# A decoder trunk in split float32 on one core: buffers, weights, latents and keys moved by bytes, and two groups of spare transposes replaced by products in two halves

## The chip, the core and the metric

The kernel runs on one core of a Trainium2 chip. Five engines work side by side on a core: TensorE (PE in the profile; its weight loads are listed apart as PEld), VectorE (DVE), ScalarE (ACT), GpSimd (POOL) and SyncE (SP, which here issues the transfers). Operands lie in the core's SBUF memory, 128 partitions wide; TensorE accumulates into PSUM, eight banks of 512 float32 a partition. The metric is the device time of one execution in microseconds, as a median over runs.

## What is computed

A trunk of two layers over 256 positions of width 1024. Cut to what matters:

```python
for i in range(2):
    if i == 1:
        k_nope, k_rope, v = shared_kv(x, kv_w_down, kv_norm, kv_w_up, cos, sin)
    x = post_norm(x, 0.5 * swiglu(x, ffn1_w_in[i], ffn1_w_out[i]), ...)   # 1024 -> 2 x 2816 -> 1024
    mix = fox_mixer(x, ...) if i == 0 else mla_mixer(x, ...)              # 16 heads each
    x = post_norm(x, mix, ...)
    x = post_norm(x, 0.5 * swiglu(x, ffn2_w_in[i], ffn2_w_out[i]), ...)
    gate = sigmoid(x @ ple_w_gate[i] + ple_b_gate[i])
    x = post_norm(x, gate * (p[i] @ ple_w_proj[i]), ...)
```

All inputs are float32. Every weight is used once per execution and streams in from HBM.

## The kernel before

**Split products.** Each float32 operand is held as two rounded halves, high and low. `mm3` (line 605) issues three matmuls for each product: high by high, high by low, low by high, into one accumulator. Weights are loaded as raw tiles of 128 x 2048, and `Stream.split` (line 226) turns each into units of 1024 columns: ScalarE writes the high half, VectorE the low half, into one of ten slots `hl0` to `hl9`, or into a buffer lent for the time (`fs`, `qk`, `ota`, `otb`, `gb`). `place` (line 221) lays a unit into its slot, high half first, low half 1024 columns (4096 bytes) later. Keys named `fv` and the first layer's `pg` begin 48 columns (192 bytes) into their slot; all other keys begin at its start. `pump`, `extra`, `ahead` and `fill` decide when the next unit is split, from a running estimate of each engine's time (`busy`).

**Where the tiles lie.** The pool stacks its tiles in the order of their first use, each as large as its largest user. In bytes of a partition: ..., `xT` 16384, `rope` 1024, two `ss` of 32, `fs` 8448, `hl0` to `hl6` 8448 each, `P` 2 x 4096, `g4` 6 x 4096, `hl7` to `hl9`, `gb` 8448, `ts` 6144, `qk` 8576, `ota` 8448, `otb` 8448, small tiles, `PT` 6144, ..., `raw`. The start addresses of the kernel before, modulo 256 bytes, are: `xT` 160; `fs`, every `hl`, `P`, `g4`, `gb` and `qk` 224; `ota` and `otb` 96; `PT` 160. (8448 is 33 times 256; the two `ss` put 64 between `xT` and what follows; `qk`, of 2144 columns, is 33.5 times 256 and puts 128 between itself and what follows.)

**Stages in order**, with their places in the profiled span: first FFN (`ffn`, "cold", to 185 us), forgetting attention (`fox`, to 300), second FFN (to 484), gate (`ple`, to 509), FFN of layer 2 with the shared latent (`kv_down`, to 694), latent attention (`mla`, to 831), last FFN (to 1015), last gate. The order of work inside `fox` and `mla` is written out by hand in the lists `FOX` and `ORDER`.

**An FFN** has eleven chunks of 256 hidden columns. In a FFN that isn't the first, `H` (chunks 0 and 1) has x stationary (`xT`) and the weight `win` moving, 512 columns wide. `HT` (line 807) has the weight stationary and `xT` moving: 256 columns, as two runs of 128 (one for each half of the rows) 8192 bytes apart; 96 matmuls a chunk. Chunks 2 to 10 come in three groups of three. In the first chunk of each group, at its second step (k = 1, b = 0), `HT` calls `what` with the next bank: four transposes of 128 columns. They are real ones where there is something to turn (`T(0)`, `T(1)`, `ple_transpose`, `kv_transpose`), and in the first FFN's second and third group (chunks 5 and 8) they turn the identity into a bank that nobody reads (`spare`, line 720). After the first and the second group `sums` (line 865) multiplies the activated chunks by combined output weights: the activation, in one of the homes `fs`, `qk`, `ota`, `otb` (in this order), is stationary, the weight moves 512 wide; 21 matmuls a chunk, four chunks a call (two and three in the first FFN). `W` closes with the remaining chunks from `g4`.

**Elsewhere.** `fox`: values in `VA`, `VB`, `VC` (keys `fv`, `fvb`, `fvc`, moving against `xT`; `fvc` with a pitch of 272 columns), keys and queries in `ws` (weight stationary, `xT` moving), output in `O` (stationary `ota`, `otb`, moving `fo`). `mla`: query latent in `dq` (moving against `xT`), turned into `cqt` (in `gb`), rotary queries in `q_rope` (stationary `cqt`, moving `qr`), values in `V` (stationary `ckv` in `fs`, moving `kvv`), and for each head `gen` (line 1689): 6 matmuls with stationary `kvk` and moving `ckv`, 9 with stationary `qn` and moving `cqt`, both 2 x 128 columns; `QK` with the rotary key `kr` (in `fs` from column 1088) moving; output in `O` (stationary `otb`, `ota`, and `fs` for the last two heads).

Of the kernel before, what the change touches and what calls it, by code (L numbers as in the profile page):

```python
# [11 lines left out]
F32R = mybir.dt.float32r  # L12
# [132 lines left out]
class Stream:  # L145
# [74 lines left out]

    def place(self, key, slot):
        w = self.pool.tile([128, 2112], F32R, tag=slot, name=slot, bufs=1)
        c = 48 if moves(key) else 0
        return w[:, c : c + 2048].rearrange("p (i c) -> p i c", i=2)

    def split(self, half=False):
        self.later()
        nc = self.nc
        key = self.order[self.ready]
        g = group_of(key)  # L230
        while self.sums_left(key):
            self.add(g)
        src, parts, n = unit_of(key, self.raw[g], self.sums.get(g))
        if self.aside(key):
            w = self.pool.tile([128, 2, 512], F32R, tag="g4", name="g4", bufs=6)
        else:
            slot = self.slots.pop(0)
            self.slot_of[key] = slot
            w = self.place(key, slot)
        hi, lo = w[:parts, 0, :n], w[:parts, 1, :n]  # L240
        shape = src.shape
        if len(shape) == 3:
            hi = hi.rearrange("p (a b) -> p a b", b=shape[2])
            lo = lo.rearrange("p (a b) -> p a b", b=shape[2])
        elif len(shape) == 4:
            hi = hi.rearrange("p (a b c) -> p a b c", b=shape[2], c=shape[3])
            lo = lo.rearrange("p (a b c) -> p a b c", b=shape[2], c=shape[3])
        t = self.arrives[group_of(key)]
        self.act_t, self.dve_t = max(self.act_t, t), max(self.dve_t, t)

        def both():
            nc.scalar.activation(hi, src, AF.Copy)  # L252
            nc.vector.tensor_tensor(lo, src, hi.bitcast(F32), op=ALU.subtract)  # L253

        if key[0] == "pb":
            nc.gpsimd.memset(w[:, 0, :].bitcast(F32), 0.0)
            lo = w[32:33, 0, :n]
            both()
        elif half:
            nc.scalar.activation(hi, src, AF.Copy)  # L260
            self.busy(act=n)

            def rest():
                nc.vector.tensor_tensor(lo, src, hi.bitcast(F32), op=ALU.subtract)  # L264
                self.busy(dve=n)
                self.split_done(key, w)

            self.rest = rest
            return
        else:  # L270
            both()
        self.pair(n)
        self.split_done(key, w)

    def aside(self, key):
# [148 lines left out]
    return key  # L424


def moves(key):
    return key[0] == "fv" or key[:2] == ("pg", 0)


def unit_of(key, raw, sums=None):

    k, u = key[0], key[-1] % 2
    if k in ("win", "fv"):
        return raw.rearrange("p (k c) -> p k c", c=512)[:, 2 * u : 2 * u + 2, :], 128, 1024
    if k == "wiu":
        return raw[:, 1024 * u : 1024 * u + 1024], 128, 1024
    if k == "ws":
        i = key[-1]
        return ((raw, sums)[i // 2])[:, 1024 * u : 1024 * u + (512 if i == 3 else 1024)], 128, 512 if i == 3 else 1024  # L440
    if k == "fvc":
        n = 816 if key[-1] < 2 else 544
        return raw[:, n * u : n * u + n], 128, n
    if k in ("wout", "fvb", "fo", "pg", "pp", "mo", "qr"):
        return raw[:, 1024 * u : 1024 * u + 1024], 128, 1024
    if k in ("fk", "fq"):
        return raw.rearrange("p (k c) -> p k c", c=256)[:, :, 128 * u : 128 * u + 128], 128, 1024
    if k == "pb":
        return raw[0:1, 0:1024], 1, 1024
    if k == "kd":  # L450
        return raw[:, 640 * u : 640 * u + 640], 128, 640
    if k == "dq":
        return raw[:, 768 * u : 768 * u + 768], 128, 768
    if k == "qn":
        return raw[:, 512:1280], 128, 768
    if k == "kvv":
        return raw[:, 0:1024], 128, 1024
    if k == "kvk":
        return raw[:, 0:512], 128, 512
    raise KeyError(key)  # L460
# [50 lines left out]
class Trunk:  # L511
# [209 lines left out]
    def ffn(self, li, which, lni, kv=False, ple=False, at=None, cold=False, after=()):  # L721


        nc, S = self.nc, self.S
# [79 lines left out]

            return f

        def HT(c, gate, up, what=None):
            for half in range(2):
                ps = self.bank(*(up if half else gate))
                for u in range(2):  # L810
                    w = self.use(("wiu", li, which, c, 2 * half + u))
                    for kk, b in ((kk, b) for kk in range(4) for b in range(2)):
                        k = 4 * u + kk
                        if (half, k, b) == (0, 1, 0) and what:
                            what(self.bank(*up))
                        col = slice(256 * kk + 128 * b, 256 * kk + 128 * b + 128)
                        self.mm3(
                            ps[:, 256 * b : 256 * b + 256], lambda i: w[:, i, col], lambda i: self.xT[:, :, i, k, :],
                            (k, b) == (0, 0), (k, b) == (7, 1),
                        )  # L820
                if half == 0:
                    gt = self.room(c, summed)
                    nc.scalar.activation(gt, ps, AF.Silu)  # L823
                    S.busy(act=512)
            close(c, gt, ps)
# [123 lines left out]
        else:  # L949
# [13 lines left out]
        n = NCH  # L963

        turns = (
            None if cold else T(0),
            self.spare if cold else T(1),
            self.kv_transpose if kv else self.ple_transpose if ple else self.spare,
        )
        x = self.turn["h"] if cold else 1 - self.turn["h"]  # L970
        for i, group in enumerate((((1,) + GROUPS[0]) if cold else GROUPS[0],) + GROUPS[1:]):
            for c in group:
                for f in at.get(c, ()):
                    f()
                if c == 2:
                    S.lend("gb")
                if c == 8:
                    S.reclaim("gb")
                if c == 10:
                    S.check("gb")  # L980
                    self.load_gb(li, lni)
                if c == 10 and kv:
                    self.kv_transpose_rope()
                if i == 0 and c == group[0]:
                    banks = ("tr", self.turn["tr"]), ("tr", 1 - self.turn["tr"])
                    turn = turns[0] and (lambda _: turns[0](self.bank("h", 1 - x)))
                    HT(c, *banks, turn)
                else:
                    HT(c, ("h", x), ("h", 1 - x), turns[i] if c == group[0] else None)
            if i < 2:  # L990
                if i == 1 and kv:
                    self.flush()
                sums([c for c in summed if (c < 5 and (cold or c != 1)) == (i == 0)], ("h", x))
                x = 1 - x
            if i == 1:
                S.lend(*after)
                combine()
# [126 lines left out]
    def fox(self, li):  # L1124
        nc, S, a = self.nc, self.S, self.a
# [26 lines left out]
        def VC(t, at={}):  # L1152

            ps = self.bank("y")
            for k in range(8):
                if k in at:
                    at[k]()
                if k % 3 == 0:
                    w = self.use(("fvc", k // 3))
                c = 272 * (k % 3)  # L1160
                self.mm3(
                    ps[:, 0:272], lambda i: self.xT[:, t, i, k, :], lambda i: w[:, i, c : c + 272], k == 0, k == 7)
            if (t, 1) not in v:
                v[t, 1] = self.tl([128, 2, 512], F32R, "g4", 6)
            o = v[t, 1]
            nc.scalar.activation(ftok[:, t, 112:128], ps[:, 256:272], AF.Copy)
            self.parts(o[:, 0, 256:512], o[:, 1, 256:512], ps[:, 0:256])
# [26 lines left out]
        f, e, u, r, ab = (fs[fr, 256 * i : 256 * i + 256] for i in range(5))  # L1194
# [79 lines left out]
        qk = self.own([128, 2, 2, 512], F32R, "qk")  # L1274
# [200 lines left out]

    def kv_transpose_rope(self):
        nc = self.nc
        self.kr = self.kvt[:, 1088:1856].rearrange("p (i t c) -> p t i c", t=2, i=3)
        kr = [self.kr[:, :, i, :] for i in range(3)]
        b = self.bank("tr")  # L1480
        for t in range(2):
# [20 lines left out]
    def mla(self, li):  # L1502
# [3 lines left out]
            self.dma(qn, pbcast(a["mla_q_norm"][0], QR))  # L1506
        scale = float(192 ** -0.5)
        v = {}
        cqt = self.tl([128, 2, 2, 3, 128], F32R, "gb", 1)
        cqtok = self.tl([128, 2, 768], F32, "PT", 1)  # L1510
        S.reclaim("otb", "qk")
        home = {}
# [163 lines left out]

        def gen(h):
            if h == 0:
                o = self.own([128, 2, 1072], F32R, "qk")
                home["qk"] = o[:, :, 0:1024].rearrange("p w (t i s c) -> p w t i s c", t=2, i=2, s=2)  # L1680
            ps = self.bank("h")
            hp, s = h // 2, h % 2
# [252 lines left out]
```

## Time and profile before

| | |
|---|---|
| median of three runs | 1050.32 us (1049.77 to 1051.04) |
| the profiled execution's own time | 1049.6 us |
| its span in the profile | 1047.8 us |
| granted TensorE clock, mean of the span | 0.998 |
| HBM read | 200.55 MB, 192 GB/s over the span |
| matmuls | 7085 |

The profile is one execution; its span runs from the first to the last profiled instruction, 1.8 us shorter than that execution's own time. In the timeline a row merges instructions of one kind on one engine: start, length, engine, line, operation, result <- operands, partitions x columns of the moving operand, and how many. A matmul's record is longer than its turn, since the next one starts before it ends: a turn is the distance from one start to the next, so a group's mean turn is the distance from its row's start to the next row's start, over its count. The chain of waits gives start, length and count of pieces without that overlap. The trace shows no addresses: distances between operands come from the program, as given above.

### The profile page before, as it was taken

The numbers are of one execution on the slowest core, as the hardware profiler recorded it, in microseconds if no ns is written. First come the engines' busy times: TensorE is split into PE (matmuls) and PEld (weight loads), VectorE is DVE, ScalarE is ACT, GpSimd is POOL, SyncE is SP. The second block draws the span as 40 slices with busy tenths as digits, with TensorE's granted clock in tenths as the row PEclk, the third lists the DMA queues.
The fourth block names the chain that finished last, engine by engine and source line by source line (L and its number), as shares of the span: only waits on it lengthen the run. The fifth ranks groups of instructions, "written<-read, shape, count | busy, mean of one in ns | idle before, by whom it ended". The sixth has DMA issues, their size and how long they took to land.

```text
span 1047.8 us, 17555 instructions
## 1 busy us (share of the span) xinstructions
PE 1035.6 (99%) x7085; PEld 948.6 (91%) x7085; DVE 891.8 (85%) x1312; ACT 592.9 (57%) x901; POOL 58.0 (6%) x88
## 2 busy tenths in 40 slices
PE   9999999999999999999999999999999999999996
PEld 8999898899889999998899898988999889898986
DVE  5788977868898979978979899888887989889877
ACT  6555563666755555663565646646776564646541
POOL 0000000122300000000220000000000000000000
PEclk9999999999999999999999999999999999999999
DMA  7855586455636363673674545743445564555732
GB/s 281 305 191 188 185 298 243 162 168 169 216 128 246 121 252 125 241 282 132 236 260 151 195 169 190 270 142 112 145 156 179 183 214 162 200 190 176 271 125 81
DMA packets 37476, 202.74 MB, mean 193 GB/s; under 512 B 3970, under 2 KB 9874, under 8 KB 16532
## 3 DMA queue, kind: packets, MB, share of 16 engines
q1 hardware_dynamic: 37396, 201.63, 54.3%
q8 instruction: 55, 0.90, 0.3%
q14 instruction: 25, 0.20, 0.1%
HBM read 200.55 MB, written 1.06 MB: 192 GB/s over the span
## 4 chain that ended last, share of the span: by engine, by line
PE 95%; DVE 2%; ACT 1%; issue 1%; DMA 0%; SPq 0%; DVEq 0%; ACTq 0%
PE h L616 53%; PE y L616 29%; PE tr L616 10%; PE tr L620 2%; DVE hl L253 1%; PE h L620 1%; DMA raw<-in_w_dram 0%; PE tr L1375 0%; DVE ts L300 0%; DVE x L705 0%; DVE tr L1720 0%; ACT qk L629 0%; DVE PT L633 0%; DVE ts L306 0%; DVE raw L308 0%
## 5 line engine op out<-in xcount | busy, mean ns | idle before, releaser
L616 PE MATMUL h<-xT,hl 128*128 128x256 f32 x3144 | 366.1, 277 | 1.2 <-ACT hl L327 0.7
L616 PEld LDWEIGHTS h<-xT,hl 128*128 128x128 f32 x3144 | 362.0, 188 | 2.9 <-ACT hl L327 1.2
L253 DVE TENSOR_TENSOR hl<-raw,hl 128x1024 fp32r<-128x1024 f32 (+5 forms) x271 | 314.2, 1190 | 36.1 <-ACT hl L252 35.0
L252 ACT ACTIVATE hl<-raw 128x1024 fp32r<-128x1024 f32 (+5 forms) x271 | 267.8, 1027 | 70.6 <-DVE raw L308 41.3
L616 PE MATMUL y<-hl,g 128*128 128x512 f32 x336 | 78.6, 391 | 0.0
L616 PEld LDWEIGHTS y<-hl,g 128*128 128x128 f32 x336 | 62.5, 188 | 12.6
L616 PE MATMUL h<-hl,xT 128*128 128x512 f32 (+2 forms) x312 | 67.9, 371 | 0.0
L616 PEld LDWEIGHTS h<-hl,xT 128*128 128x128 f32 x312 | 54.9, 188 | 9.8
L616 PE MATMUL y<-hl,otb 128*128 128x512 f32 x219 | 58.0, 399 | 0.0
L264 DVE TENSOR_TENSOR hl<-raw,hl 128x1024 fp32r<-128x1024 f32 (+2 forms) x44 | 52.3, 1192 | 0.8 <-ACT hl L260 0.7
L616 PE MATMUL y<-hl,xT 128*128 128x512 f32 (+3 forms) x282 | 52.7, 334 | 0.0
L260 ACT ACTIVATE hl<-raw 128x1024 fp32r<-128x1024 f32 (+2 forms) x44 | 45.2, 1029 | 9.7 <-DVE raw L308 9.1
L629 ACT ACTIVATE xT<-tr 128x512 fp32r<-128x512 f32 x28 | 16.1, 597 | 58.9 <-PE tr L620 58.9
L616 PEld LDWEIGHTS y<-hl,xT 128*128 128x128 f32 x282 | 44.1, 188 | 4.6 <-ACT xT L629 0.4
L616 PEld LDWEIGHTS y<-hl,otb 128*128 128x128 f32 x219 | 39.8, 188 | 8.4 <-DVE otb L633 0.3
L616 PE MATMUL y<-hl,ota 128*128 128x512 f32 x177 | 46.8, 398 | 0.1
L700 POOL TENSOR_TENSOR rs<-ve,mhalf 128x1 f32<-128x1 f32 x16 | 15.1, 942 | 519.8 <-DVE ve L699 519.8
L616 PE MATMUL tr<-xT,hl 128*128 128x256 f32 x360 | 42.5, 277 | 0.0
L616 PEld LDWEIGHTS tr<-xT,hl 128*128 128x128 f32 x360 | 41.7, 188 | 0.4
L616 PEld LDWEIGHTS y<-hl,ota 128*128 128x128 f32 x177 | 32.7, 189 | 7.7 <-DVE hl L253 0.6
L823 ACT ACTIVATE P<-h 128x512 f32<-128x512 f32 x33 | 19.7, 596 | 33.0 <-PE h L616 32.6
L300 DVE TENSOR_TENSOR ts<-raw 128x1024 f32<-128x1024 f32 x29 | 35.4, 1222 | 0.6
(322 smaller groups left out, 1632.7 us busy)
## 6 DMA issues: line engine op xcount, KB each, us to landing
raw<-in_ffn_in_dram SPq DMA_DIRECT2D x85, 1024.0 KB, 5.0
raw<-in_ffn_out_dram SPq DMA_DIRECT2D x44, 1024.0 KB, 5.0
raw<-in_pg_dram SPq DMA_DIRECT2D x8, 1024.0 KB, 4.9
raw<-in_mo_dram SPq DMA_DIRECT2D x8, 1024.0 KB, 4.8
raw<-in_kq_dram SPq DMA_DIRECT2D x8, 640.0 KB, 4.2
gb<-in_ln_g_dram SPq DMA_DIRECT2D x8, 512.0 KB, 5.9
gb<-in_ln_b_dram SPq DMA_DIRECT2D x8, 512.0 KB, 7.5
raw<-in_fk_dram SPq DMA_DIRECT2D x4, 1024.0 KB, 5.6
```

The lines of the kernel that those rows point to most:

```text
L252: nc.scalar.activation(hi, src, AF.Copy)
L253: nc.vector.tensor_tensor(lo, src, hi.bitcast(F32), op=ALU.subtract)
L260: nc.scalar.activation(hi, src, AF.Copy)
L264: nc.vector.tensor_tensor(lo, src, hi.bitcast(F32), op=ALU.subtract)
L300: tt(s[:, 0:1024].rearrange("p (a b) -> p a b", b=512), r[:, 0:512][:, None, :].to_broadcast([128, 2, 512]), r[:, 512:1536].rearrange("p ( ...
L616: self.nc.tensor.matmul(out, lhsT, rhs, start=start, stop=stop)
L620: self.nc.tensor.transpose(out, in_, self.ident)
L629: self.nc.scalar.activation(hi, src, AF.Copy)
L700: nc.gpsimd.tensor_tensor(rs, ve, self.mhalf, op=ALU.pow)
L823: nc.scalar.activation(gt, ps, AF.Silu)
```

## The change

It has four parts. First, every unit of some keys begins further into its slot: 48 columns for `kvv`, `qr` and all `win` but the first FFN's, 32 for `fvb` and `fvc`, 36 for `kd`, 40 for `dq`; the columns of `fvc` are laid with a pitch of 320 where it was 272. Second, `cqt` begins 48 columns into `gb`, and `kr` 32 columns further into `fs`. Third, the `qk` tile is declared 2176 columns long where it was 2144 (its inner pitch stays 1072), so all tiles stacked behind it move by 128 bytes. Fourth, `spare` is no longer called from `HT`; in the first FFN's chunks 5 and 8 the matmul high by high of step k = 1, b = 0 is issued as two of 128 columns, one for each half of the rows, with the same weights.

```diff
     def place(self, key, slot):
         w = self.pool.tile([128, 2112], F32R, tag=slot, name=slot, bufs=1)
-        c = 48 if moves(key) else 0
+        c = shift(key)
         return w[:, c : c + 2048].rearrange("p (i c) -> p i c", i=2)
...
         if len(shape) == 3:
-            hi = hi.rearrange("p (a b) -> p a b", b=shape[2])
-            lo = lo.rearrange("p (a b) -> p a b", b=shape[2])
+            b = n // shape[1]
+            hi = hi.rearrange("p (a b) -> p a b", b=b)[:, :, 0 : shape[2]]
+            lo = lo.rearrange("p (a b) -> p a b", b=b)[:, :, 0 : shape[2]]
...
-        self.pair(n)
+        self.pair(math.prod(shape[1:]))
...
-def moves(key):
-    return key[0] == "fv" or key[:2] == ("pg", 0)
+def shift(key):
+
+    if key[0] in ("fv", "kvv", "qr") or key[:2] == ("pg", 0) or key[0] == "win" and key[1:3] != (0, "ffn1"):
+        return 48
+    return {"fvb": 32, "fvc": 32, "kd": 36, "dq": 40}.get(key[0], 0)
...
     if k == "fvc":
         n = 816 if key[-1] < 2 else 544
-        return raw[:, n * u : n * u + n], 128, n
+        return raw[:, n * u : n * u + n].rearrange("p (a b) -> p a b", b=272), 128, n // 272 * 320
...
-        def HT(c, gate, up, what=None):
+        def HT(c, gate, up, what=None, halve=False):
...
                         col = slice(256 * kk + 128 * b, 256 * kk + 128 * b + 128)
+                        if halve and (half, k, b) == (0, 1, 0):
+                            o = ps[:, 0:256]
+                            for t in range(2):
+                                self.mm(o[:, 128 * t : 128 * t + 128], w[:, 0, col], self.xT[:, t, 0, k, :], False, False)
+                            self.mm(o, w[:, 0, col], self.xT[:, :, 1, k, :], False, False)
+                            self.mm(o, w[:, 1, col], self.xT[:, :, 0, k, :], False, False)
+                            S.pump()
+                            continue
...
         turns = (
             None if cold else T(0),
-            self.spare if cold else T(1),
-            self.kv_transpose if kv else self.ple_transpose if ple else self.spare,
+            None if cold else T(1),
+            self.kv_transpose if kv else self.ple_transpose if ple else None,
         )
...
-                    HT(c, ("h", x), ("h", 1 - x), turns[i] if c == group[0] else None)
+                    HT(c, ("h", x), ("h", 1 - x), turns[i] if c == group[0] else None, c == group[0] and not turns[i])
...
-                c = 272 * (k % 3)
+                c = 320 * (k % 3)
...
-        self.kr = self.kvt[:, 1088:1856].rearrange("p (i t c) -> p t i c", t=2, i=3)
+        self.kr = self.kvt[:, 1120:1888].rearrange("p (i t c) -> p t i c", t=2, i=3)
...
-        cqt = self.tl([128, 2, 2, 3, 128], F32R, "gb", 1)
+        cqt = self.tl([128, 1584], F32R, "gb", 1)[:, 48:1584].rearrange("p (t i k c) -> p t i k c", t=2, i=2, k=3)
...
-                o = self.own([128, 2, 1072], F32R, "qk")
+                o = self.own([128, 2176], F32R, "qk")[:, 0:2144].rearrange("p (w c) -> p w c", w=2)
```

## The prediction

> **What bounds the kernel now.** I read the page first: busy times, then the chain that ended last.
>
> ```profile
> span 1047.8 us, 17555 instructions
> PE 1035.6 (99%) x7085; PEld 948.6 (91%) x7085; DVE 891.8 (85%) x1312; ACT 592.9 (57%) x901; POOL 58.0 (6%) x88
> ...
> PE 95%; DVE 2%; ACT 1%; issue 1%; DMA 0%; SPq 0%; DVEq 0%; ACTq 0%
> ```
>
> TensorE is busy for 99% and makes 95% of the chain. The kernel therefore gets faster only if matmuls are fewer or their turns shorter, and the change takes out only eight transposes. So I went on to the turns: the distance from start to start in the timeline. First the output products of the second FFN, 21 of 512 columns for each home, as the stationary operand changes from `fs` to `qk`, `ota` and `otb` (timeline of TensorE, the first row of each home and the row behind the last):
>
> ```profile
> 356.36 1.54 PE L616 MATMUL y<-gb,fs 128*128 128x512 f32 x6
> ...
> 361.13 1.52 PE L616 MATMUL y<-hl,qk 128*128 128x512 f32 x6
> ...
> 365.90 1.56 PE L616 MATMUL y<-hl,ota 128*128 128x512 f32 x6
> ...
> 370.78 1.56 PE L616 MATMUL y<-hl,otb 128*128 128x512 f32 x6
> ...
> 375.65 0.87 PE L616 MATMUL h<-xT,hl 128*128 128x256 f32 x6
> ```
>
> The four homes take 4.77, 4.77, 4.88 and 4.87 us: 227 ns a turn with `fs` and `qk`, 232 with `ota` and `otb`. The work is the same; what differs is the address. I call **distance** the start of the next stationary operand less the start of the moving one, modulo 256 bytes. The moving weight lies in a slot (224), so the distance is 0 with `fs` and `qk` (224) and 128 with `ota` and `otb` (96). Two pieces of the chain of waits add distance 192 (`H`: `xT` at 160 against a slot) and a long stretch at 0 (`W` and its neighbours):
>
> ```profile
> 300.53 8.24 PE h L616 x36
> ...
> 467.25 14.97 PE y L616 x66
> ```
>
> That is 228.9 and 226.8 ns. For 512 columns: 0 is best, 192 costs 2 ns, 128 costs 5. With 256 columns one distance can have two speeds. In the attention's key and query products (distance 64, timeline):
>
> ```profile
> 210.12 2.99 PE L616 MATMUL h<-xT,hl 128*128 128x256 f32 x24
> 212.95 0.38 PE L620 MATMUL tr<-ident,fs 128*128 128x128 f32 x2
> ...
> 239.97 5.62 PE L616 MATMUL h<-xT,hl 128*128 128x256 f32 x48
> 245.43 2.88 PE L616 MATMUL h<-xT,otb 128*128 128x256 f32 x24
> 248.15 0.60 PE L1375 MATMUL tr<-ident,P 128*128 128x128 f32 x4
> 248.58 0.38 PE L620 MATMUL tr<-ident,P 128*128 128x128 f32 x2
> 248.72 3.07 PE L616 MATMUL h<-xT,hl 128*128 128x256 f32 x24
> 251.63 0.62 PE L616 MATMUL h<-PT,g 128*128 128x512 f32 x2
> ```
>
> The 24 from 210.12 take 117.9 ns each, the 48 from 239.97 take 113.8, and 24 more 113.3; behind six transposes the 24 from 248.72 take 121 (the first of them is long). So there is a short and a long **pace**, and each lasts until something disturbs it. The first layer shows what the spare transposes do about it (timeline, then the chain):
>
> ```profile
> 70.92 0.87 PE L616 MATMUL h<-xT,hl 128*128 128x256 f32 x6
> 71.63 0.60 PE L620 MATMUL h<-ident 128*128 128x128 f32 x4
> 71.98 1.51 PE L616 MATMUL h<-xT,hl 128*128 128x256 f32 x11
> ```
>
> ```profile
> 72.23 26.55 PE h L616 x234
> ```
>
> Six products at 118 ns, four transposes, and then 234 at 113.5.
>
> **The change part by part.** The sum is made against the profiled execution: 1049.6 us, of which the span is 1047.8; the median is 0.7 above the former, and I take the difference off the median.
>
> *`qk` longer by 128 bytes.* `ota` and `otb` move from 96 to 224, distance 128 to 0. In `sums` 13 chunks of 21 products have these homes (four in each of three FFNs, one in the first): 13 x 0.105 us (4.875 less 4.77) = **1.37**. In `fox` the output product runs 96 times from these homes, in `mla` 168 times. There the runs are short, and a run at distance 0 needs some products to settle; the rows below are of one head in `mla`, six with `otb`, six with `fs`:
>
> ```profile
> 786.10 1.56 PE L616 MATMUL y<-hl,otb 128*128 128x512 f32 x6
> 787.49 1.53 PE L616 MATMUL tr<-hl,fs 128*128 128x512 f32 x6
> 788.87 0.40 PE L616 MATMUL h<-PT,g 128*128 128x256 f32 x2
> ```
>
> 231.7 against 230. So `mla` gains 168 x 1.7 = **0.29** (at most 168 x 4.9 = 0.8); `fox`, with longer runs, 96 x 3.3, between the two, = **0.32**. `HT` weights in `ota` and `otb` go from 192 to 64; the 24 from 245.43 (`otb`, 192) run at 113.3 as those of the short pace at 64 do: nothing.
>
> *`win` by 192 bytes.* 96 products in each of three FFNs go from distance 192 to 0: 288 x (228.9 - 226.8) = 0.60; less some for settling: **0.50**.
>
> *`cqt`.* In `gen` nine products a head have `cqt` moving, at distance 0, after six with `ckv` at 64:
>
> ```profile
> 734.84 0.85 PE L616 MATMUL h<-fs,hl 128*128 128x256 f32 x6
> 735.53 1.22 PE L616 MATMUL h<-gb,hl 128*128 128x256 f32 x9
> 736.59 0.35 PE L616 MATMUL tr<-qk 128*128 128x256 f32 x2
> 736.77 0.33 PE L616 MATMUL tr<-fs,xT 128*128 128x256 f32 x1
> 736.95 0.52 PE L616 MATMUL tr<-qk 128*128 128x256 f32 x3
> ```
>
> The six take 115 each and the nine 117.8. At 192 bytes more the nine stand at 64 like the six. All at the short pace: 144 x (117.8 - 113.5) = 0.62; all at the long one: nothing. Six of them at 115 on average say that they reach the short one within about three: **0.45**. `qr` moves by as much as `cqt`, so its distance stays 0.
>
> *The small ones.* `kvv` (48 products, 192 or 64 to 0), `fvb`, `fvc`, `kd`, `dq` (48 each, to 64, 64, 48 and 32), the rotary key (48), the products with `PT` (96), the values' and first gate's products in `otb` (24). Distances 32 and 48 stand in no row of this trace, and for these widths neither does 64 in a run of its own. The bounds are the 5 ns between best and worst above, in either direction: 408 x 5 = 2.0 us down or up. The last gate has 96 products of 256 columns:
>
> ```profile
> 1027.85 0.84 PE L616 MATMUL y<-hl,xT 128*128 128x256 f32 x6
> 1028.53 0.52 PE L616 MATMUL y<-otb,xT 128*128 128x256 f32 x3
> 1028.88 0.52 PE L616 MATMUL y<-qk,xT 128*128 128x256 f32 x3
> ```
>
> Six at 113, and from the unit in `otb` on 117; with `otb` at the distance of the others the break has no cause, worth up to 90 x 4 = 0.36. I take **0.6** for all of this, nearest to the rows of `kvv` and the gate, which have known ends.
>
> *The transposes.* Between 71.63 and 71.98 pass 0.35 us, and the eleven after them end at 73.49; at 0.28 us a record the last began at 73.21, ten turns in 1.23, 0.1 more than at the short pace. So four cost 0.45 us. A product of 128 columns saves nothing beside one of 256: in the `QK` rows above, products of 256, 128 and 256 columns take 0.36 us from 736.59 to 736.95, three full turns of 120. So the halving adds one turn, 0.12, and saves 0.33, twice: **0.66**. What it must keep is the pace: if the group stays at the long one, 282 products at 4.5 ns cost 1.27 us a group. In `QK`, too, such a product upsets the even succession of turns, so I take it to be enough. Issue estimates in `pump` shift by some 0.3 us, which can move single splits on ScalarE and VectorE; there is slack for that nearly everywhere in the first layer but the stretch shown next.
>
> *At no cost:* the shifts, the pitch and the longer tile add no instruction, no wait and no transfer, and the splits on ScalarE and VectorE keep their element counts; nothing on SP's or POOL's queue moves. Without the spare transposes the second bank is first claimed where its products begin, half a chunk later, so a wait there can only become shorter.
>
> **What takes some back.** The sum is 1.37 + 0.29 + 0.32 + 0.50 + 0.45 + 0.60 + 0.66 = 4.2 us. Not all of it ends up in the span, for VectorE is close behind in places. Windows over the second call of `sums` in the second FFN and over the heads of `mla` (columns: window, its length, then PE, PEld, DVE, ACT and POOL busy):
>
> ```profile
> 409.20:428.20 19.00, 19.00 (x84) 15.54 (x84) 18.62 (x23) 10.31 (x13) 0.00 (x0) 1.00 0.45 154
> 716.00:831.50 115.50, 114.97 (x756) 103.65 (x755) 99.45 (x235) 79.76 (x191) 0.92 (x1) 1.00 0.44 152
> ```
>
> VectorE is at 98% in the former. There its low half ends 0.23 us before TensorE reads it (timeline, the unit in `gb`):
>
> ```profile
> 421.98 1.22 DVE L253 TENSOR_TENSOR gb<-raw,gb 128x1024 fp32r<-128x1024 f32 x1
> ...
> 423.43 1.10 PE L616 MATMUL y<-gb,otb 128*128 128x512 f32 x4
> ```
>
> Up to there this call wins about 0.15, so it just holds. In the first layer it doesn't (chain of waits):
>
> ```profile
> 95.93 2.85 PE h L616 x25
> ...
> 112.93 1.15 DVE hl L253
> ...
> 114.12 1.42 PE y L616 x5
> ```
>
> TensorE already waits for VectorE there, so the one chunk with `ota` wins nothing (0.1 lost); the time of the transposes at 71.6 does pass, since this chain starts from the matmuls that end at 98.78. In `fox` and `mla` softmax steps on ScalarE and VectorE stand between a head's products; I let 7 parts in 10 of their gains pass, of `sums` 9, of the halving 8.5, of the small ones 7.5, of `win` all. That gives 1.23 + 0.20 + 0.22 + 0.50 + 0.32 + 0.45 + 0.56 = **3.5 us: 1046.8**.
>
> **The rivals.** *1. Distances cost nothing.* Then the four homes would differ for some other reason, and only the transposes count: 0.56, **1049.8**. The row with four equal sets of work speaks against it, and so does `fs` against `otb` within one head. The Trainium skill, page "TensorE: Matmul & The Clock Gate", section "Step-by-step: what each phase is for", has this rule: "Loading the next tile's weights doesn't steal SBUF read bandwidth from the running matmul." By it no address could matter; the trace's 232 against 227 ns disagrees. *2. VectorE takes back more.* Where it is at 98%, the gain of `sums` goes into waiting, and half of `fox` and `mla` as well: 1.23 and some 0.4 less, **1048.4**. For it speaks the 0.23 us of slack, against it that VectorE's work waits for TensorE's slots outside these calls. *3. The halves don't set the short pace.* The two groups of the first layer run at 118: 2 x 1.27 more, **1049.3**. The attention's 248.72 row speaks for it: the six transposes ahead of it turned the short pace into the long one. *4. More falls into the short pace*, 0.9 for the attention's keys and queries (384 products, half of them at the long pace now), 0.4 for `gen` and the gate, 0.8 of the small ones' bound: **1044.7**. *5. Slower:* the nine groups of the later FFNs, which keep their transposes, are entered from quicker stretches and stay at the long pace, at 1.27 us each. From three groups on the gain is gone, from five the kernel is slower by over 0.2%; six give **1054.4**. Against it: the six products before these transposes run at 118 now as well, so the entry isn't new.
>
> **How the numbers follow.** Forecast 0.54; rival 1 0.06, 2 0.13, 3 0.12, 4 0.10, 5 0.05. A measurement of this kernel can tell about 0.2%, 2.1 us, from no change, so faster means under 1048.2. The forecast and rival 4 lie there, and about a half of rival 2, whose price is uncertain by as much: 0.72. Rivals 1, 3 and the rest of 2 are within 0.2%: 0.22. Slower: rival 5 and a little for unknown distances that turn out bad, 0.06. The range from 1044.4 to 1049.4 takes in rivals 2, 3 and 4 and the small ones' 2 us either way beside a gain of 3.5; it leaves out rivals 1 and 5 and a tail below.
>
> **What would show it.** Each of the 13 chunks with `ota` or `otb` takes 4.77 us where it took 4.88; `H` shows 36 products in under 8.2 us; the nine `cqt` products in `gen` take about 1.03 us, not 1.06; the page has eight fewer transposes and two more matmuls (7079); chunks 5 and 8 of the first FFN run at 113.5 ns from the third product after the halves. Wrong would be: `ota` chunks still at 4.88 (distance isn't the cause), stretches of `HT` at 118, or TensorE waits behind VectorE that have grown by the gain.

## The result and the profile after

The changed kernel took 1056.57 us (median of six runs, 1054.52 to 1059.27), the kernel before 1050.47 (six runs, 1049.12 to 1051.04): 1.006 times the time, interval 1.0044 to 1.0076. It is slower by 6.1 us, where 3.5 us less was forecast; neither the range nor any rival holds it.

The page of the changed kernel, its span and busy times:

```profile
span 1055.0 us, 17547 instructions
PE 1034.0 (98%) x7079; PEld 948.1 (90%) x7079; DVE 892.4 (85%) x1312; ACT 594.0 (56%) x901; POOL 58.1 (6%) x88
```

TensorE is busy for 1.6 us less than before (1035.6), as the shorter turns want it, and the span is 7.2 us longer. So the loss is not in the products but in time in which TensorE stands still. Where, the windows tell. Below is the stage of the latent attention, from its first product to its last, in each kernel (columns: window, its length, then PE, PEld, DVE, ACT and POOL busy, granted clock, DMA share, GB/s); first the kernel before, then the changed one:

```profile
694.39:831.67 137.28, 136.71 (x867) 122.72 (x866) 116.01 (x265) 88.78 (x209) 3.00 (x4) 1.00 0.43 150
```

```profile
693.93:839.54 145.61, 137.39 (x867) 122.28 (x866) 116.67 (x265) 89.48 (x209) 3.01 (x4) 1.00 0.41 141
```

This stage alone is 8.33 us longer. TensorE stood still for 137.28 - 136.71 = 0.57 us in it before, and stands still for 8.22 now. The clock is the same, and so is the number of instructions on each engine. Most other stages, taken the same way, became shorter: the three later FFNs 1.43 us together, the last gate 0.43, the first gate 0.09. The forgetting attention is 0.02 longer and the first FFN 0.43, whose chunks 2 to 4 fell into the long pace in the changed kernel (rows at experiment 7).

What TensorE waited for, summed over the span (waiting engine, tile and line, releaser: us in total, times, longest), in the changed kernel:

```profile
PE tr L620 <- DVE qk L637: 5.2, 4, 1.8
PE tr L620 <- ACT qk L633: 2.3, 3, 1.3
PE h L620 <- ACT hl L328: 1.2, 2, 0.9
```

The same view of the kernel before begins:

```profile
PE y L592 <- POOL mhalf L577: 1.2, 1, 1.2
PE h L616 <- ACT hl L327: 0.7, 1, 0.7
```

Seven waits for `qk`, 7.5 us, are new: the head's `QK` (result `tr`) stands behind a write of `qk` by ScalarE or VectorE. The longest but one is at 752.93. The timeline of the changed kernel there (start, length, engine, line, operation, result <- operands, count, and in brackets the idle time before and its releaser):

```profile
750.66 0.49 PE L624 MATMUL tr<-ident,P 128*128 128x128 f32 x3
...
750.86 0.60 ACT L633 ACTIVATE qk<-h 128x512 fp32r<-128x512 f32 x1 [0.21 <-PE h L620]
...
752.10 0.68 DVE L637 TENSOR_TENSOR qk<-h,qk 128x512 fp32r<-128x512 f32 x1
...
752.93 0.42 PE L620 MATMUL tr<-qk 128*128 128x256 f32 x2 [1.78 <-DVE qk L637]
```

And the same place in the kernel before:

```profile
750.78 0.49 PE L620 MATMUL tr<-ident,P 128*128 128x128 f32 x3
...
750.98 0.60 ACT L629 ACTIVATE qk<-h 128x512 fp32r<-128x512 f32 x1 [0.23 <-PE h L616]
...
751.03 0.43 PE L616 MATMUL tr<-qk 128*128 128x256 f32 x2
...
752.23 0.68 DVE L633 TENSOR_TENSOR qk<-h,qk 128x512 fp32r<-128x512 f32 x1
```

Before, the product that reads `qk` starts at 751.03, while ScalarE is writing `qk` (750.98 to 751.58) and 1.2 us ahead of VectorE's write. That is right, because they touch different columns: `ORDER` has `gen 6`, `ga 6`, `T 4`, `ta 4`, `td 4`, `gd 6` and then `QK 5`, so the writes (`ga`, `gd`) are those of head 6, and the product reads head 5. Even and odd heads lie in alternating blocks of 128 columns. After, the product starts 0.15 us behind the end of VectorE's write of head 6. The same instructions stand in the same order; the product of one head now waits for the queries and keys of the next.

What brings this wait is the way in which the longer tile was declared. `[128, 2, 1072]` became a flat `[128, 2176]`, of which the first 2144 columns are taken and regrouped in two rows of 1072. Between the kernel before and the same kernel with this one line changed (experiment 2 below), the instruction lists differ in the waits of 25 matmuls. Ten of them belong to `QK`, which now waits for a later write of `qk` than before; the other 15 stand behind these, and 14 of them only lost a wait that the earlier one covers. In the other direction two writes of `qk` by ScalarE and two by VectorE now wait for a later product of `QK`. The program's dependency tracking no longer keeps the interleaved blocks apart when the view is a part of a longer tile. Why it can't is a matter of that software and stays open; a flat tile of exactly 2144 columns gives the waits of before in the instruction list, though it wasn't run. In `ORDER` the next head's `ga` stands ahead of `QK` for eleven of sixteen heads, so the case is the rule; where the write has long ended, the wait costs nothing. Seven of the ten show as standing time in the trace.

### The profile page after: what moved, and what is told of

The parts are those of the page before. It is cut to its first block, busy times and chain, and to the rows that moved or that the text cites. A ratio compares the mean times of both kernels' runs of the same rounds, so it can differ in the third digit from the quotient of the medians.

```text
span 1055.0 us, 17547 instructions
## 1 busy us (share of the span) xinstructions
PE 1034.0 (98%) x7079; PEld 948.1 (90%) x7079; DVE 892.4 (85%) x1312; ACT 594.0 (56%) x901; POOL 58.1 (6%) x88
## 4 chain that ended last, share of the span: by engine, by line
PE 65%; DVE 5%; ACT 2%; issue 1%; DVEq 0%; ACTq 0%
PE h L620 34%; PE y L620 21%; PE tr L620 8%; PE tr L624 2%; DVE hl L254 1%; ACT qk L633 1%; DVE ts L301 0%; PE h L624 0%; ACT hl L253 0%; DVE tr L1732 0%; DVE qk L637 0%; DVE ts L307 0%; DVE raw L309 0%; DVE g L254 0%; ACT P L1742 0%
## 5 line engine op out<-in xcount | busy, mean ns | idle before, releaser
L254 DVE TENSOR_TENSOR hl<-raw,hl 128x1024 fp32r<-128x1024 f32 (+4 forms) x272 | 315.5, 1191 | 37.4 <-ACT hl L253 36.2
L253 ACT ACTIVATE hl<-raw 128x1024 fp32r<-128x1024 f32 (+4 forms) x272 | 268.8, 1027 | 72.0 <-DVE raw L309 41.4
```

## The experiments

The theory: the new wait makes the whole loss, and without it the change gains about what was forecast. Its main rivals: the new addresses cost time in the latent attention, or the planner's shifted estimates moved a split to a bad place.

**1. The change with the waits of before.** `qk` as before; the 128 bytes stand in a small tile of their own ahead of `ota`, so every address is that of the changed kernel, and all five engines have its instructions in its order.

```diff
     def own(self, shape, dt, tag):
         self.S.check(tag)
+        if tag == "ota":
+            self.tl([128, 32], F32, "gap4", 1)
...
-                o = self.own([128, 2176], F32R, "qk")[:, 0:2144].rearrange("p (w c) -> p w c", w=2)
+                o = self.own([128, 2, 1072], F32R, "qk")
```

> The changed kernel with the qk tile declared 128 x 2 x 1072 as before, and a tile of 32 columns that nobody uses behind it: every address is that of the changed kernel, and the waits of the latent attention are those of the kernel before. Theory (false waits: in the longer flat tile a head's QK also waits for the next head's queries and keys): the eight matmul waits in the latent attention, 7.5 us in the changed kernel's trace, fall below 1 us, and the time is 1056.6 - 7.5 to 8.3 = 1048.3 to 1049.1. Rival (the moved addresses slow something in that stage): it stays at 1055 to 1057.

Measured: 1046.45 us (1045.28 to 1048.11) against 1050.02 for the kernel before on the same chip, ratio 0.9968 (0.9957 to 0.998). Windows over the latent attention, then the first rows of what TensorE waited for:

```profile
692.98:829.35 136.37, 135.70 (x867) 122.24 (x866) 116.01 (x265) 88.75 (x209) 3.01 (x4) 1.00 0.43 151
```

```profile
PE y L598 <- POOL mhalf L583: 1.2, 1, 1.2
PE h L622 <- DVE PT L639: 0.7, 2, 0.6
```

The waits for `qk` are gone, the stage takes 9.24 us less than in the changed kernel, and TensorE stands still in it for 0.67. Addresses and order are the same, so both rivals fall. Of the 9.24, 7.55 are standing time; the other 1.69 are busy time (137.39 against 135.70) with the same matmuls. Compared start by start, the two traces show where: from the product ahead of each of the seven waits to the `QK` behind it, the changed kernel takes 9.01 us more in all (2.03 at 752.93, where it stands still for 1.78). The record of the product ahead, longer than its turn, runs on into the wait and counts as busy. So the seven waits make 9.0 of the 9.24.

The whole came out some 2 us lower than the theory had it, which took off the standing time alone. Besides the latent attention, two stages are shorter than in the changed kernel: the forgetting attention by 0.62 us (its 360 key and query products at 256 columns take 41.73 us against 42.37, at the short pace for longer) and the first FFN by 0.35. The two programs are the same in both stages, so that is scatter of the pace and of the start, of which more below, and not the wait.

**2. The kernel before with the long tile alone.**

```diff
-                o = self.own([128, 2, 1072], F32R, "qk")
+                o = self.own([128, 2176], F32R, "qk")[:, 0:2144].rearrange("p (w c) -> p w c", w=2)
```

> The kernel before with nothing but the qk tile declared as 2176 flat columns. Theory (false waits): it has the same waits in the latent attention as the changed kernel, costs 8 us there and gains 1.5 to 2 us from ota and otb at distance 0: 1056 to 1057. Rival (the shifts of weights and latents make the loss): 1048 to 1049, below the kernel before.

Measured: 1056.83 us (1055.61 to 1059.12), ratio 1.0069 (1.0055 to 1.0084). The latent attention, and what TensorE waited for:

```profile
694.49:840.37 145.88, 137.77 (x868) 122.73 (x867) 116.62 (x265) 89.56 (x209) 3.01 (x4) 1.00 0.40 141
```

```profile
PE tr L616 <- DVE qk L633: 5.2, 4, 1.8
PE tr L616 <- ACT qk L629: 2.3, 3, 1.2
```

This one line brings the same waits, to the tenth of a microsecond (7.5 us), and the whole loss. It also moves `ota` and `otb`, as experiment 3 does with the waits of before; there the stage takes 136.84 us:

```profile
692.11:828.95 136.84, 136.25 (x868) 122.71 (x867) 116.03 (x265) 88.81 (x209) 3.01 (x4) 1.00 0.43 150
```

With all addresses alike, the declaration costs this stage 145.88 - 136.84 = 9.04 us.

**3. The kernel before with the 128 bytes alone,** as the small tile ahead of `ota`, with the waits of before: the buffers' distances by themselves.

```diff
     def own(self, shape, dt, tag):
         self.S.check(tag)
+        if tag == "ota":
+            self.tl([128, 32], F32, "gap4", 1)
```

> The kernel before with nothing but 128 unused bytes between qk and ota, so ota, otb and what lies behind them move as in the change, with the waits of before. Theory (false waits): a chunk of the output products with ota or otb takes 4.77 us where it took 4.88; the time is 1050.5 - 1.5 to 2.0 = 1048.5 to 1049. Rival (the moved buffers make the loss): 1055 or more. Rival (distances cost nothing): 1050.5.

Measured: 1046.57 us (1045.68 to 1048.32), ratio 0.9972 (0.9961 to 0.9984), 3.45 us less by the medians. The second FFN's chunks with `ota` and `otb` (timeline of TensorE):

```profile
364.49 1.52 PE L618 MATMUL y<-hl,ota 128*128 128x512 f32 x6
...
369.25 1.52 PE L618 MATMUL y<-hl,otb 128*128 128x512 f32 x6
...
374.01 0.87 PE L618 MATMUL h<-xT,hl 128*128 128x256 f32 x6
```

4.76 us each, where the same work took 4.88 and 4.87: only addresses differ, so the address is the cause. That the distance to the moving operand counts, and not `ota`'s own address, is borne out by `win`: there the moving operand was shifted and `xT` stayed, and the turn changed too (below). The gain is more than the 1.5 to 2.0 expected. Part of it is the start: a wait for the first weights ends at 7.06 us here and at 7.61 before, chunk 2 begins at 27.89 against 28.75, and the first FFN's stage is 0.93 shorter (182.03 against 182.96). Next to nothing of that comes from `ota`, which this stage's `sums` uses for one chunk behind chunk 2.

**4. Experiment 1 with the spare transposes in place of the halves.**

```diff
-            None if cold else T(1),
-            self.kv_transpose if kv else self.ple_transpose if ple else None,
+            self.spare if cold else T(1),
+            self.kv_transpose if kv else self.ple_transpose if ple else self.spare,
```

(With it `HT` is no longer called with `halve`.)

> The first kernel of this set with the four spare transposes back in the first layer's chunks 5 and 8 in place of the halves. Theory (a product in two halves sets the short pace as well as four transposes and is 0.33 us shorter): 0.66 us slower than the first kernel of this set. Rival (the halves disturb the order of splits and cost as much): equal within 0.3 us, or faster.

Measured: 1046.66 us (1045.46 to 1047.4), ratio 0.9968 (0.9956 to 0.9981). By time it can't be told from experiment 1; by the trace it can, as the next shows.

**5. Experiment 1 with neither halves nor transposes.**

```diff
-                    HT(c, ("h", x), ("h", 1 - x), turns[i] if c == group[0] else None, c == group[0] and not turns[i])
+                    HT(c, ("h", x), ("h", 1 - x), turns[i] if c == group[0] else None)
```

> e1_exact_waits with neither halves nor spare transposes in the first layer: chunks 5 and 8 begin like any others. Theory (the pace lasts until something disturbs it, and only the halves change it): chunks 5 to 7 and 8 to 10 run at 118 ns a product and take 33.9 us each where they take 32.78 with the halves; the time is 1046.5 + 2.2 = 1048.7. Rival (the pace finds itself back without help): 0.24 us faster than e1_exact_waits, since two turns of 0.12 us are gone.

Measured: 1048.0 us (1047.77 to 1050.62), ratio 0.9985 (0.9976 to 0.9995). The group of chunks 5 to 7 (timeline of TensorE), first with neither:

```profile
70.53 2.99 PE L622 MATMUL h<-xT,hl 128*128 128x256 f32 x24
...
76.19 28.43 PE L622 MATMUL h<-xT,hl 128*128 128x256 f32 x240
104.45 1.52 PE L622 MATMUL y<-gb,fs 128*128 128x512 f32 x6
```

then with the halves (experiment 1):

```profile
71.80 3.03 PE L622 MATMUL h<-xT,hl 128*128 128x256 f32 x25
...
77.38 27.36 PE L622 MATMUL h<-xT,hl 128*128 128x256 f32 x240
104.58 1.54 PE L622 MATMUL y<-gb,fs 128*128 128x512 f32 x6
```

and with the transposes (experiment 4):

```profile
70.47 0.87 PE L622 MATMUL h<-xT,hl 128*128 128x256 f32 x6
71.18 0.60 PE L626 MATMUL h<-ident 128*128 128x128 f32 x4
...
103.60 1.54 PE L622 MATMUL y<-gb,fs 128*128 128x512 f32 x6
```

From the group's first row to the first `y<-gb,fs`: 33.92 us with neither (117.8 ns a turn all through), 32.78 with the halves (113.3 from 77.38 on), 33.13 with the transposes. One product in two halves sets the short pace for the some 280 that follow and costs 0.35 us less than the four transposes. By such rows the two groups together take 2.3 us more with neither, as expected (2.2); the medians differ by 1.55.

**6. Experiment 1 with more halves and `kd` at distance 0.** `kd` is shifted by 48 columns, not 36, and two more products are halved: in the first FFN's chunk 2, and in the forgetting attention's first key product.

```diff
-    return {"fvb": 32, "fvc": 32, "kd": 36, "dq": 40}.get(key[0], 0)
+    return {"fvb": 32, "fvc": 32, "kd": 48, "dq": 40}.get(key[0], 0)
...
-(..., c == group[0] and not turns[i])
+(..., c == group[0] and not turns[i] or cold and c == 2)
...
+                if key == ("fk", 0) and k == 1:
+                    s = slice(128, 256)
+                    for t in range(2):
+                        self.mm(out[:, 128 * t : 128 * t + 128], w[:, 0, s], self.xT[:, t, 0, k, :], False, False)
...
```

> e1_exact_waits with the kd units 48 columns into their slot (distance 0, where 36 gave 48) and two more products in halves: in the first layer's chunk 2 and in the first key product of the forgetting attention. Theory: kd turns go from 153 to 142 ns, 0.5 us less; chunks 2 to 4 are at 113.5 ns whatever the start did to them (0 to 1.1 us less); the first keys and queries go from 118 to 113.5 ns, 0.3 us less after the cost of the halves: 1045.1 to 1046.0. Rival (320 columns have no better distance, and other work gives it back): 1046.5.

Measured: 1046.1 us (1045.35 to 1047.51), ratio 0.9963 (0.9951 to 0.9976): the lowest median of the study, 3.9 us under the kernel before, but not to be told from experiment 1, and just above the range expected. The 24 products of `kd` share a row with 18 of `H`. It begins and ends so in the changed kernel (distance 48), then here (0):

```profile
508.91 7.94 PE L620 MATMUL h<-hl,xT 128*128 128x320 f32 x42
516.68 1.52 PE L620 MATMUL h<-otb,xT 128*128 128x512 f32 x6
```

```profile
509.00 7.78 PE L622 MATMUL h<-hl,xT 128*128 128x320 f32 x42
516.62 1.52 PE L622 MATMUL h<-otb,xT 128*128 128x512 f32 x6
```

7.77 us against 7.62, 6 ns a product of `kd`. At distance 192, before, one took 147 ns; it takes 153 at 48 and 147 again at 0, not the 142 expected. The first keys' pace gained nothing from their halves (the 20 products behind them take 117.1 ns each, the 24 in this place of experiment 1 117.9): a halved product doesn't set the short pace everywhere.

**7. The kernel before with the shifts, `cqt`, `kr` and the pitch alone** (all of `shift`, the `fvc` pitch and the moved `cqt` and `kr`, with `qk`, `ota`, `otb` and their waits as before).

```diff
-        c = 48 if moves(key) else 0
+        c = shift(key)
...
-        cqt = self.tl([128, 2, 2, 3, 128], F32R, "gb", 1)
+        cqt = self.tl([128, 1584], F32R, "gb", 1)[:, 48:1584].rearrange("p (t i k c) -> p t i k c", t=2, i=2, k=3)
...
```

> The kernel before with the shifts of the units, of cqt and of the rotary key and the pitch of fvc alone: no byte is moved behind qk, the waits are those of before, the spare transposes are there. Theory: the weights in H, the latent's nine products a head and V gain 1.1 to 1.5 us, kd loses 0.3: 1049 to 1049.7, with ota and otb still at 4.88 us a chunk. Rival (the shifts cost something that the other runs hide): 1050.5 or more.

Measured: 1048.13 us (1047.87 to 1049.3) against 1050.02, ratio 0.9987 (0.9978 to 0.9995), a little under the range expected. The chunks with `ota` and `otb` are as before, 4.88 and 4.87 us (timeline of TensorE):

```profile
365.32 1.56 PE L620 MATMUL y<-hl,ota 128*128 128x512 f32 x6
...
370.20 1.56 PE L620 MATMUL y<-hl,otb 128*128 128x512 f32 x6
...
375.07 0.87 PE L620 MATMUL h<-xT,hl 128*128 128x256 f32 x6
```

The parts don't add up by the medians: experiment 3 gains 3.45 us and this one 1.9, and experiment 1, which has both and the halves, 3.6. Each interval is about 2 us wide, and one cause of the scatter can be seen. Chunks 2 to 4 of the first FFN fall into one pace or the other, though no edit but experiment 6 touches their products. In the kernel before (timeline of TensorE):

```profile
28.75 27.36 PE L616 MATMUL h<-xT,hl 128*128 128x256 f32 x240
55.95 2.88 PE L616 MATMUL h<-xT,gb 128*128 128x256 f32 x24
```

and in the changed one:

```profile
28.69 28.43 PE L620 MATMUL h<-xT,hl 128*128 128x256 f32 x240
56.96 2.99 PE L620 MATMUL h<-xT,gb 128*128 128x256 f32 x24
```

27.20 us against 28.27 for the same 240 products. Of the experiments, only 2 came out at the long one. That is why the parts are weighed by their rows below, and the medians only for what is larger.

## Why the prediction was wrong, point by point

**The step that failed** is the one under "At no cost": "the shifts, the pitch and the longer tile add no instruction, no wait and no transfer". The longer tile adds waits at `QK`, worth 9.04 us of stage time by themselves (145.88 in experiment 2 against 136.84 in experiment 3, with the same addresses), and this turns a gain into a loss. The prediction weighed the tile by its bytes alone. Its declaration also changes from which view the dependencies are made, and the list of `QK` and `ORDER` was at hand: a writer that stands right ahead of a reader of the same tile, and that the trace of before shows running at the same time as it (750.98 and 751.03). None of the rivals had this. Rival 5, the slower one, gave a time near the result (1054.4) by a mechanism that didn't occur: no group of the later FFNs stayed at the long pace.

**The sum.** Without the wait, experiment 1 gives 1046.45 us, ratio 0.9968, where 1046.8 was forecast; 3.6 us by the medians, for 3.5. So the rest of the working holds as a whole, though the close agreement is in part luck. The interval runs from 2.1 to 4.5 us, and the first FFN begins its chunk 2 at 29.62 us in experiment 1 and at 28.75 before, ahead of any product that the change touches. Against that, a gain came in that no term held. TensorE no longer stands still ahead of the first transposes in the forgetting attention, as it does before:

```profile
193.08 0.63 PE L620 MATMUL tr<-ident,x 128*128 128x128 f32 x4 [0.33 <-issue]
```

In experiment 1:

```profile
192.66 0.60 PE L626 MATMUL tr<-ident,x 128*128 128x128 f32 x4
```

From the 12 products ahead of these transposes to the transposes it takes 2.00 us before and 1.47 to 1.48 without the standing. The standing is there in every kernel with the spare transposes (before, experiments 2, 3, 4 and 7) and gone in every one without them (the changed one, experiments 1, 5 and 6), so their absence ends it; by which wait wasn't traced.

The terms, from the sums over the same rows before and after (or in experiment 1, where the wait disturbs them in the changed kernel):

- *`sums`, 0.105 a chunk:* 0.12 measured. The second FFN's chunks in the changed kernel (timeline of TensorE):

```profile
366.17 1.52 PE L620 MATMUL y<-hl,ota 128*128 128x512 f32 x6
...
370.93 1.52 PE L620 MATMUL y<-hl,otb 128*128 128x512 f32 x6
...
375.69 0.87 PE L620 MATMUL h<-xT,hl 128*128 128x256 f32 x6
```

  4.76 us each, for 4.77 forecast; the eight chunks of a FFN, four of them with `ota` or `otb`, went from 38.59 to 38.11, in each of the three.
- *Outputs:* `fox` 0.36 (22.84 to 22.48) for 0.32; `mla` 0.49 over the 168 products (40.23 to 39.74), both in experiment 1, for 0.29. The one pair of rows that it was sized by had shown too little.
- *`win`:* 0.59 for 0.50. In the changed kernel (timeline of TensorE, the second FFN):

```profile
300.81 2.91 PE L620 MATMUL h<-hl,xT 128*128 128x512 f32 x12
...
309.00 1.03 PE L624 MATMUL tr<-ident,x 128*128 128x128 f32 x8
```

  36 products in 8.19 us, 8.25 before by the same reading.
- *`cqt`:* 0.52 in `gen` (29.72 to 29.20 in experiment 1) for 0.45.
- *The small ones:* 0.6 taken, and mixed in fact. The last gate gave 0.41 (22.26 to 21.85): it now keeps the short pace through the unit in `otb`, where it broke off before (timeline of TensorE, changed kernel):

```profile
1035.09 0.84 PE L620 MATMUL y<-hl,xT 128*128 128x256 f32 x6
1035.77 0.50 PE L620 MATMUL y<-otb,xT 128*128 128x256 f32 x3
1036.11 0.50 PE L620 MATMUL y<-qk,xT 128*128 128x256 f32 x3
```

  113 ns a turn in the first two rows. The first gate gave 0.10, `kvv` 0.12, `fvb` 0.08 and `fvc` 0.07 (the standing above left out). `kd` lost 0.3 over its 48 products, `QK` 0.1, and `dq` didn't change (8.81 to 8.84). Distance 48 was one that no row of the trace of before showed. The products with `PT` weren't weighed.
- *The halves:* 0.35 a group for 0.33. They keep the short pace, so rival 3 falls.

**What was passed on.** The three later FFNs gained 2.03 us in the rows of `sums` and `win` and lost 0.3 in `kd`; their stages became 1.43 shorter. That is eight parts in ten, about what the sum had let pass. Rival 2, which let VectorE take all of `sums` back, falls: the second call gained as much as the first. What the FFNs' rows and stages differ by wasn't traced further.

**Rival 1,** that distances cost nothing, falls with experiment 3. The rule of the Trainium skill quoted beside it (page "TensorE: Matmul & The Clock Gate", section "Step-by-step: what each phase is for"), that loading the next weights doesn't steal read bandwidth from the running matmul, disagrees with this trace, if it is taken to mean that the start of those weights can't matter: 21 products took 4.88 us or 4.76 with nothing of theirs moved but the stationary operand's start. By which way the start acts, no run here shows.

## What to carry to other kernels

A tile's declared shape is part of the schedule: where one engine writes interleaved blocks of a tile while another reads its neighbours, look in the timeline for such overlapping pairs, and move the tile with padding outside it rather than by lengthening it. When an edit is costed at nothing, compare the waits of the two programs and not only their instructions. An engine that is less busy in a longer span points at a new wait; the windows find its stage and the waits view its name.

## What the runs showed of the hardware

- The start of the next stationary operand against the moving one, modulo 256 bytes, sets the turn of a 512-column product (the slots lie odd and even multiples of 256 bytes apart and give the same turn): 226.7 ns at distance 0 and 232 at 128, with `ota` and `otb` moved by 128 bytes and nothing else of these products changed (experiment 3; in experiment 7, where they stay, it is 232). For 320 columns it is 147 at 0 and at 192, but 153 at 48.
- At 256 columns the same operands run at either of two paces, 113.3 and 117.8 ns, and keep it for 240 products and more. One product in two halves of 128 columns switched from the long pace to the short one in both groups of the first FFN, but not for the first keys of the forgetting attention. What sets the pace after a wait stays open.
